# Building the state-space tables of a hybrid encoder block on one engine: two tables in one set of operations, half of a third one mirrored

## The chip, the cores and the metric

The kernel runs on one core of a Trainium2 chip. The metric is the device time of one execution in microseconds (us); the kernel before takes 1011.92 us, the median of three runs (1011.55 to 1013.5). The engines are named as in the profile: PE (TensorE matmuls; PEld its weight loads), DVE (VectorE), ACT (ScalarE), POOL (GpSimd) and SP (the queue that issues most transfers).

## The reference

One layer, one sequence of 1024 tokens, model width 1024. Two branches share one input projection: differential attention with 4 heads, and a bidirectional S5 state-space branch. Only the second is touched here:

```python
# 2 directions, 32 groups of 16 channels, 64 complex states each
mag = exp(lr * dt); ab = mag * (cos(li*dt) + i sin(li*dt))      # the state matrix's diagonal a
bb  = coef[..., None] * b                                        # input matrix
bu  = einsum('bsgh,gph->sbgp', u, bb)
x   = associative_scan(x[s] = a * x[s-1] + bu[s])                # per direction, one reversed
y   = einsum('sbgp,ghp->bsgh', x_re, c_re) - einsum('sbgp,ghp->bsgh', x_im, c_im)
```

The sum over both directions goes through D*u, GELU, a gate and an up-projection, is merged with the attention branch, and a last projection, residual and RMSNorm give the output.

## The kernel before

The program is written as generators that are stepped in an order fixed by hand: every engine runs its own instructions in program order. `drive(main, fill)` steps a main generator; each number that it yields is a budget of PE time, and that much of a second generator, `fill`, is put into the program at that place. The fill of the state-space stage are projection units: 48 matmuls each (16 steps of three, 0.66 of budget a step) that have nothing to do with the state-space work. Each unit's weights are split into a high part (ACT, tile `wh`) and a low part (in this stage DVE, tile `wl`) when the unit before it starts. So PE has work wherever the main line waits for another engine, as far as the budgets reach, and waits where they end.

The state-space work has two parts.

`startup` prepares parameters (`params_a` to `params_d`, `put_tabs`). `params_b` makes small tables of powers of a on DVE: `wn` (8 powers), `rbn` (16) and `ran` (8) unit rotations, the last from nine squarings (`e_pow`). `params_d` multiplies b by the coefficients (`bb`, six complex-product steps on POOL) and by a rotation (`bq`, six on DVE); `put_tabs` copies the tables with ACT to `wt`, `rb`, `ra`, with the second 64 partitions (the reversed direction) in reversed order; four ACT copies fill `bz` from `bb`.

`ssm_main` then handles eight blocks of four groups. A token index is split in 8 by 128 (T=8, NJ=128): within the 8 a small table does the work, over the 128 a scan. For block i:

- `stage_a`: three outer products of 128x512 elements, as six element-wise operations each (real and imaginary part: two products and a sum). `ba` (the B table, bq times wt) is made on DVE, `ca` (the C table, ct times wt) and `rr` (the rotation table, ra times rb) on POOL. ACT fills `rt`, POOL sets two of its columns.
- `stage_b`: PE transposes `ba` (tile `tp`), ACT copies the result to `gt`.
- `stage_k`: PE multiplies `bz` by `ca` (tile `kp`), ACT copies `kp` to `kt`, DVE and ACT form `kf` from it; by way of DRAM it comes back as the Toeplitz tile `m`.
- `stage_c`: PE multiplies `gt` by the input `ut` (PSUM tile `w`), DVE turns it by `rr` (six operations), runs four scans (`sb`) and two small memsets.
- `stage_d`: DVE turns the scans back by `rr` (six operations on `z` and `t`).
- `stage_e`: PE sums `m` times `ut` and `ca` times `z` (tile `yp`), ACT writes `ys`, and it goes to DRAM.

The order of the main line in iteration i is: stage_a(i+1), input load of i+1, stage_c(i), fill YA (4.4), stage_b(i+1), stage_e(i-1), fill YB (4.6), stage_d(i), stage_k(i+1), fill YC (4.6). So DVE's order in one iteration is ba(i+1), turning and scans of i, z of i, kf(i+1), with `wl` wherever a new unit starts; PE's order is w(i), YA, tp(i+1), yp(i-1), YB, kp(i+1), YC. Ahead of the loop stand stage_a(0), a fill of 7.0, stage_b(0), a fill of 5.0 and stage_k(0). The helper `tt` (L60) issues nearly all element-wise operations, and `act` (L81) all of ACT's, so the tiles' names tell them apart.

## Time and profile before

| | before |
|---|---|
| median of three runs | 1011.92 us |
| the profiled execution's own time | 1012.06 us |
| its span, first to last instruction | 1010.2 us |
| PE busy | 901.7 us (89%) |
| DVE busy | 710.0 us (70%) |
| POOL busy | 393.2 us (39%) |
| ACT busy | 375.9 us (37%) |
| granted PE clock, mean | 0.944 |
| chain that ended last | PE 52%, DVE 27%, ACT 6%, DMA 5% |

The shares are means over stages that differ. The startup lasts to about 120 us, the state-space stage with its fill from there to about 395 us; attention and the output projection follow. A row of the trace gives the start of an instruction, its duration, engine, line, operation and tiles; in brackets stands the idle time of the engine before it and what ended it. Where two operations of an engine follow each other closely, their durations overlap a little, and the distance of their starts is what the second costs.

### The profile page before, as it was taken

Reading aid. Unit: us, or ns where it says so; the run is one execution under the profiler, and the core shown is the slowest. Engines: PE = TensorE matmul, PEld = TensorE weight load, DVE = VectorE, ACT = ScalarE, POOL = GpSimd, SP = SyncE. Lnnn points to the kernel's source line nnn. Section 1 sums busy time; section 2 is a strip of 40 time slices with the busy share of each in tenths; the row PEclk is TensorE's granted clock in tenths of the full one; section 3 lists DMA queues with packets and bytes.
Section 4 is the critical chain, followed back from the end, with each engine's and each line's share of the span. In section 5 each row is a group of like instructions: output and inputs, shape, how many; then the busy total and the mean of one; then the engine's idle time right before and its main releaser. Section 6 shows DMA issues by size and latency. Waiting matters only on the chain.

```text
span 1010.2 us, 12306 instructions
## 1 busy us (share of the span) xinstructions
PE 901.7 (89%) x4532; PEld 751.3 (74%) x4532; DVE 710.0 (70%) x1179; ACT 375.9 (37%) x647; POOL 393.2 (39%) x250
## 2 busy tenths in 40 slices
PE   4699968588677799999989999899989999999997
PEld 3577856477566588787868888788878888788886
DVE  4984968999999987765646655856766563565455
ACT  5434351112111115511245545545545644332222
POOL 3433279876766801422226334515601110331000
PEclk9789988798777889999999999999999999999999
DMA  9744213022421425686343312131240231675212
GB/s 303 190 124 124 85 55 102 21 71 71 130 58 47 138 81 167 209 285 235 84 115 74 94 42 74 43 102 34 63 115 21 72 97 63 241 259 207 105 63 104
DMA packets 105326, 115.38 MB, mean 114 GB/s; under 512 B 7459, under 2 KB 87568, under 8 KB 105266
## 3 DMA queue, kind: packets, MB, share of 16 engines
q1 hardware_dynamic: 103476, 109.88, 35.6%
q10 hardware_dynamic: 1614, 4.51, 1.1%
q8 instruction: 36, 0.59, 0.2%
q0 software_dynamic: 176, 0.20, 0.1%
q14 instruction: 24, 0.20, 0.1%
HBM read 76.36 MB, written 25.63 MB: 101 GB/s over the span
## 4 chain that ended last, share of the span: by engine, by line
PE 52%; DVE 27%; ACT 6%; DMA 5%; issue 4%; POOL 3%; SPq 2%; DVEq 0%; ACTq 0%; POOLq 0%
PE mm L202 27%; PE op L1843 8%; PE pv L1614 4%; DVE ba L60 4%; DVE z L60 2%; PE sc L1573 2%; DVE tv L60 2%; PE sc L1572 2%; DVE acc L78 2%; PE tp L1603 2%; DVE t L60 2%; PE u L785 1%; DVE sb L1174 1%; DVE sb L1172 1%; DVE wl L60 1%
## 5 line engine op out<-in xcount | busy, mean ns | idle before, releaser
L202 PE MATMUL mm<-hh,wh 128*128 128x512 f32 x592 | 240.5, 406 | 0.6 <-ACT o L81 0.6
L202 PE MATMUL mm<-hl,wh 128*128 128x512 f32 x592 | 233.8, 395 | 0.0
L202 PE MATMUL mm<-hh,wl 128*128 128x512 f32 x592 | 233.3, 394 | 0.0
L60 POOL TENSOR_TENSOR wl<-wr,wh 128x1024 fp32r<-128x1024 f32 x28 | 74.7, 2667 | 289.7 <-ACT wh L81 287.9
L202 PEld LDWEIGHTS mm<-hh,wh 128*128 128x128 f32 x592 | 113.5, 192 | 24.0 <-issue 1.4
L202 PEld LDWEIGHTS mm<-hh,wl 128*128 128x128 f32 x592 | 112.8, 191 | 24.6
L202 PEld LDWEIGHTS mm<-hl,wh 128*128 128x128 f32 x592 | 113.2, 191 | 21.4
L60 DVE TENSOR_TENSOR wtl<-tp,wth 128x512 fp32r<-128x512 f32 x64 | 41.2, 686 | 101.1 <-ACT wth L81 101.1
L81 ACT ACTIVATE e<-sc,nm 128x1024 f32<-128x1024 f32 x64 | 71.4, 1116 | 98.3 <-DVE nm L1574 98.3
L1574 DVE TENSOR_REDUCE nm<-sc 128x1 f32<-128x1024 f32 x64 | 75.3, 1217 | 10.5 <-PE sc L1573 10.3
L1116 PE MATMUL tp<-cst,ba 128*128 128x128 f32 x64 | 16.9, 418 | 61.3 <-DVE ba L60 61.3
L81 ACT ACTIVATE wh<-wr 128x1024 fp32r<-128x1024 f32 x48 | 50.7, 1056 | 40.2 <-DMA pad<-pt 21.2
L1116 PEld LDWEIGHTS tp<-cst,ba 128*128 128x128 f32 x64 | 11.1, 212 | 67.3 <-issue 58.1
L1573 PE MATMUL sc<-kk,qb 128*128 128x512 f32 x128 | 50.3, 393 | 2.8 <-DMA qb<-qq 2.8
L1843 PE MATMUL op<-woh,ml 128*128 128x512 f32 (+1 forms) x136 | 51.7, 380 | 0.1
L1843 PE MATMUL op<-wol,mh 128*128 128x512 f32 (+1 forms) x136 | 51.6, 379 | 0.0
L1843 PE MATMUL op<-woh,mh 128*128 128x512 f32 (+1 forms) x136 | 51.6, 379 | 0.0
L1572 PE MATMUL sc<-kk,qq 128*128 128x512 f32 x128 | 50.2, 392 | 0.5 <-issue 0.5
L81 ACT ACTIVATE side<-mm 128x512 f32<-128x512 f32 x40 | 23.8, 595 | 68.0 <-PE mm L202 65.6
L78 DVE SCALAR_TENSOR_TENSOR e<-e,wm 128x1024 f32<-128x1024 f32 x32 | 47.1, 1472 | 1.1
L60 DVE TENSOR_TENSOR wl<-wr,wh 128x1024 fp32r<-128x1024 f32 x21 | 33.7, 1605 | 18.6 <-ACT wh L81 18.4
L60 POOL TENSOR_TENSOR ca<-ct,wt 128x512 f32<-128x512 f32 x16 | 28.0, 1750 | 39.2 <-PE yp L1200 34.3
(372 smaller groups left out, 2050.0 us busy)
## 6 DMA issues: line engine op xcount, KB each, us to landing
wr<-in_w_in_dram SPq DMA_DIRECT2D x40, 512.0 KB
wa<-in_w_ada_dram SPq DMA_DIRECT2D x16, 512.0 KB
x<-in_x_dram SPq DMA_DIRECT2D x8, 512.0 KB
gsd<-side SPq DMA_DIRECT2D x8, 512.0 KB
gad<-side SPq DMA_DIRECT2D x8, 512.0 KB
gt<-gsd SPq DMA_DIRECT2D x8, 512.0 KB
wg<-in_w_ada_dram SPq DMA_DIRECT2D x8, 512.0 KB
pad<-pt ACTq DMA_DIRECT2D x8, 512.0 KB
```

The source lines that it names most:

```text
L60: (e or V).tensor_tensor(out=o, in0=a, in1=b, op=op)
L78: V.scalar_tensor_tensor(out=o, in0=a, scalar=s, in1=b, op0=op0, op1=op1)
L81: A.activation(out=o, in_=i, func=f, **kw)
L202: PE.matmul(out=ps, lhsT=a[:, k, off:off + P], rhs=r[:, k, sl], start=(n == 0), stop=(n == 3 * K - 1))
L785: PE.matmul(out=upd[2 * b + hf], lhsT=w[:, k, :], rhs=r[:, k, hf * 512:hf * 512 + 512], start=(k == 0 and p == 0), stop=(k == KD - 1 and p ...
L1116: PE.transpose(ps[:, c4 * P:c4 * P + P], ba[:, q, c4].rearrange("p t h -> p (t h)"), ident)
L1572: PE.matmul(out=sc[:, sl], lhsT=H["qq"][:, cc, tok], rhs=H["kk"][:, cc, sl], start=True, stop=False)
L1573: PE.matmul(out=sc[:, sl], lhsT=qb_t[g // 2][:, cc, tb], rhs=H["kk"][:, cc, sl], start=False, stop=True)
L1574: V.tensor_reduce(out=nm[:, cc:cc + 1], in_=sc, axis=AX.X, op=ALU.max, negate=True)
L1603: PE.transpose(ps[:, k, :], e[:, kt * P:kt * P + P], ident)
L1614: PE.matmul(out=ps[:, 0:256], lhsT=a[:, kt, :], rhs=r[:, kt, :], start=(n == 0), stop=(n == 23))
L1843: PE.matmul(out=ps[:, 0:n], lhsT=a[:, k, tok], rhs=r[:, k, lo:lo + n], start=(i == 0), stop=(i == 23))
```

## The change

- In `stage_a` all three tables are made on DVE. B and C go through one set of six operations of 128x1024 elements: their sources lie interleaved in one tile `bc` (tile `bct`, last index 0 for B, 1 for C), and the result is one tile `cb`, interleaved too. PE reads `cb[..., 0]` and `cb[..., 1]`, each second element. Of `rr` DVE makes half (128x256 elements, six operations), and two ACT operations write the other half in reversed order, the imaginary part with its sign changed. POOL keeps the two small memsets.
- `ran` and `ra` shrink from 8 to 4 entries, with one squaring less; `put_tabs` changes signs instead of order for `rb` and `ra` (eight ACT operations for six).
- `bb` in `params_d` moves from POOL to DVE. Signs that were in `ct` move into `bz` and into stages c and d (an add for a sub and the reverse).
- `stage_k` loses the copy `kt`: DVE and ACT read `kp` in PSUM.
- `gt` has one buffer for two, `cb` three as `ca` had; `tv` shares a buffer with `t1`.

```diff
+            es, half = [], []
 
             def e_pow():
                 cur = (co, sn)
                 t0 = sb("et0")
-                for q in range(9):
+                for q in range(8):
                     nxt = (sb(f"er{q}"), sb(f"ei{q}"))
                     yield from csq(nxt[0], nxt[1], cur[0], cur[1], t0)
                     cur = nxt
                     if q >= 2:
                         es.append(nxt)
+                    if q == 1:
+                        half.append(nxt)
...
-            def r_tab(tab, q, tmp):
-                seed(tab, es[q])
-                yield from grow(tab, 2, es[q + 1], tmp)
-                yield from grow(tab, 4, es[q + 2], tmp)
-                if tab is rbn:
-                    yield from grow(tab, 8, es[3], tmp)
+            def r_tab(tmp):
+                seed(rbn, es[0])
+                for q in range(3):
+                    yield from grow(rbn, 2 << q, es[q + 1], tmp)
+
+            def h_tab(tmp):
+                for q in range(2):
+                    V.tensor_copy(out=ran[:, q, 0], in_=half[0][q])
+                yield from grow(ran, 1, es[4], tmp)
+                yield from grow(ran, 2, es[5], tmp)
...
-            ra = sp.tile([P, 2, 8, 32], F32, name="ra")
-            for dst, nm in ((wt, "wn"), (rb, "rbn"), (ra, "ran")):
+            ra = sp.tile([P, 2, 4, 32], F32, name="ra")
+            act(wt[0:64], small["wn"][0:64], AF.Copy)
+            act(wt[64:P], small["wn"][64:P, :, ::-1, :], AF.Copy)
+            yield 4.0
+            for dst, nm in ((rb, "rbn"), (ra, "ran")):
                 src = small[nm]
-                act(dst[0:64], src[0:64], AF.Copy)
-                act(dst[64:P], src[64:P, :, ::-1, :], AF.Copy)
-                yield 4.0 if dst is wt else 0.1
+                act(dst[:, 0], src[:, 0], AF.Copy)
+                act(dst[0:64, 1], src[0:64, 1], AF.Copy)
+                act(dst[64:P, 1], src[64:P, 1], AF.Copy, scale=-1.0)
...
-                act(ct[:, i], ps[:].rearrange("p (g h) -> p g h", h=16), AF.Copy, scale=(1.0 if i == 0 else -1.0))
+                act(bc_[:, i, :, :, 1], ps[:].rearrange("p (g h) -> p g h", h=16), AF.Copy)
...
-            bq = sp2[0].tile([P, 2, 32, 16], F32, name="bq")
-            cmul(bb[:, 0], bb[:, 1], bs[:, 0], bs[:, 1], bc(small["cr"][:], 1, shp), bc(small["ci"][:], 1, shp), tbig, G)
-            cmul(bq[:, 0].rearrange("p g h -> p h g"), bq[:, 1].rearrange("p g h -> p h g"), bb[:, 0], bb[:, 1],
+            cmul(bb[:, 0], bb[:, 1], bs[:, 0], bs[:, 1], bc(small["cr"][:], 1, shp), bc(small["ci"][:], 1, shp), tbig, V)
+            cmul(bc_[:, 0, :, :, 0].rearrange("p g h -> p h g"), bc_[:, 1, :, :, 0].rearrange("p g h -> p h g"), bb[:, 0], bb[:, 1],
...
-                    act(bz[64 * d:64 * d + 64, i, :, d, :], bb[64 * d:64 * d + 64, i].rearrange("p h g -> p g h"), AF.Copy)
-            tabs.update(bq=bq)
+                    act(bz[64 * d:64 * d + 64, i, :, d, :], bb[64 * d:64 * d + 64, i].rearrange("p h g -> p g h"), AF.Copy,
+                        scale=1.0 - 2.0 * i)
...
-        def outer(o, br, bi, wr, wi, im_sign, tmp, e):
-            mul(o[:, 0], br, wr, e)
-            mul(tmp, bi, wi, e)
-            tt(o[:, 0], o[:, 0], tmp, ALU.subtract if im_sign > 0 else ALU.add, e)
-            mul(o[:, 1], bi, wr, e)
-            mul(tmp, br, wi, e)
-            tt(o[:, 1], o[:, 1], tmp, ALU.add if im_sign > 0 else ALU.subtract, e)
+        def outer(o_r, o_i, br, bi, wr, wi, tmp):
+            mul(o_r, br, wr)
+            mul(tmp, bi, wi)
+            sub(o_r, o_r, tmp)
+            mul(o_i, bi, wr)
+            mul(tmp, br, wi)
+            add(o_i, o_i, tmp)
 
         def stage_a(i):
             g = slice(4 * i, 4 * i + 4)
-            ca = hb.tile([P, 2, 4, 8, 16], F32, tag="ca", bufs=3, name="ca")
+            cb = hb.tile([P, 2, 4, 8, 16, 2], F32, tag="cb", bufs=3, name="cb")
             rr = hb.tile([P, 2, 4, 8, 16], F32, tag="rr", bufs=2, name="rr")
-            ba = hb.tile([P, 2, 4, 8, 16], F32, tag="ba", bufs=1, name="ba")
-            tg = hb.tile(s4, F32, tag="tg", bufs=1, name="tg")
-            tv = hb.tile(s4, F32, tag="tv", bufs=1, name="tv")
+            tv = hb.tile([P, 4, 8, 32], F32, tag="t1", bufs=1, name="tv")
             rt = hb.tile([P, 4, P], F32, tag="rt", bufs=2, name="rt")
-
-            def wv(q):
-                return bc(wt[:, q, :, g].rearrange("p k g -> p g k"), 3, s4)
-
-            outer(ba, bc(bq[:, 0, g], 2, s4), bc(bq[:, 1, g], 2, s4), wv(0), wv(1), 1, tv, V)
-            outer(ca, bc(ct[:, 0, g], 2, s4), bc(ct[:, 1, g], 2, s4), wv(0), wv(1), -1, tg, G)
-            rv = [bc(ra[:, q, :, g].rearrange("p k g -> p g k"), 3, s4) for q in range(2)]
-            rw = [bc(rb[:, q, :, g].rearrange("p k g -> p g k"), 2, s4) for q in range(2)]
-            outer(rr, rv[0], rv[1], rw[0], rw[1], 1, tg, G)
+            sc, sr = [P, 4, 8, 32], [P, 4, 4, 16]
+            bv = [bc(bct[:, q, g].rearrange("p g h x -> p g (h x)"), 2, sc) for q in range(2)]
+            wv = [bc(wt[:, q, :, g].rearrange("p k g -> p g k"), 3, sc) for q in range(2)]
+            cf = cb[:].rearrange("p q g t h x -> p q g t (h x)")
+            outer(cf[:, 0], cf[:, 1], bv[0], bv[1], wv[0], wv[1], tv)
+            rv = [bc(ra[:, q, :, g].rearrange("p k g -> p g k"), 3, sr) for q in range(2)]
+            rw = [bc(rb[:, q, :, g].rearrange("p k g -> p g k"), 2, sr) for q in range(2)]
+            outer(rr[:, 0, :, 4:8], rr[:, 1, :, 4:8], rv[0], rv[1], rw[0], rw[1], tv[:, :, 0:4, 0:16])
+            for q in range(2):
+                f = rr[:, q].rearrange("p g a b -> p g (a b)")
+                act(f[:, :, 0:64][:, :, ::-1], f[:, :, 64:P], AF.Copy, scale=1.0 - 2.0 * q)
             act(rt, bc(r8[:, g], 2, [P, 4, P]), AF.Copy)
             G.memset(rt[0:64, :, 0:1], 0.0)
             G.memset(rt[64:P, :, P - 1:P], 0.0)
-            st_[i] = dict(ca=ca, rr=rr, ba=ba, rt=rt)
+            st_[i] = dict(cb=cb, rr=rr, rt=rt)
...
-            gt = hb.tile([P, 2, 4, P], F32, tag="gt", bufs=2, name="gt")
+            cb = d["cb"]
+            gt = hb.tile([P, 2, 4, P], F32, tag="gt", bufs=1, name="gt")
             for q in range(2):
                 ps = psw.tile([P, 512], F32, tag="tp", bufs=2, name="tp")
                 for c4 in range(4):
-                    PE.transpose(ps[:, c4 * P:c4 * P + P], ba[:, q, c4].rearrange("p t h -> p (t h)"), ident)
+                    PE.transpose(ps[:, c4 * P:c4 * P + P], cb[:, q, c4, :, :, 0].rearrange("p t h -> p (t h)"), ident)
...
-                              rhs=ca[:, q, c4].rearrange("p t h -> p (t h)"), start=(q == 0), stop=(q == 1),
+                              rhs=cb[:, q, c4, :, :, 1].rearrange("p t h -> p (t h)"), start=(q == 0), stop=(q == 1),
                               tile_position=(0, 32 * c4))
-            kt = hb.tile([P, P], F32, tag="kt", bufs=1, name="kt")
             kf = hb.tile([P, 240], F32, tag="kf", bufs=1, name="kf")
-            act(kt, kp, AF.Copy)
-            V.stream_shuffle(out=kf[:, 0:P], in_=kt, mask=SWAP16)
-            act(kf[:, P:240], kt[:, 16:P], AF.Copy)
-            add(kf[:, 112:P], kf[:, 112:P], kt[:, 0:16])
+            V.stream_shuffle(out=kf[:, 0:P], in_=kp, mask=SWAP16)
+            act(kf[:, P:240], kp[:, 16:P], AF.Copy)
+            add(kf[:, 112:P], kf[:, 112:P], kp[:, 0:16])
...
-            mul(wv[:, 1], wp[1], rre)
-            mul(t1, wp[0], rim)
+            mul(wv[:, 1], wp[0], rim)
+            mul(t1, wp[1], rre)
...
-            sub(z[:, 0], z[:, 0], t1)
+            add(z[:, 0], z[:, 0], t1)
             mul(z[:, 1], sv[:, 1], rre)
             mul(t1, sv[:, 0], rim)
-            add(z[:, 1], z[:, 1], t1)
+            sub(z[:, 1], z[:, 1], t1)
...
-                    PE.matmul(out=yp[:, c4, :], lhsT=ca[:, q, c4].rearrange("p t h -> p (t h)"),
+                    PE.matmul(out=yp[:, c4, :], lhsT=cb[:, q, c4, :, :, 1].rearrange("p t h -> p (t h)"),
```

## Rows read from the trace of the kernel before

**Rows 1.** Windows (busy us by engine, granted clock, DMA): an iteration, a later stretch.

```profile
303.01:333.12 30.11, 23.07 (x124) 19.55 (x123) 29.58 (x30) 5.52 (x10) 20.64 (x15) 0.83 0.23 66
...
400.00:450.00 50.00, 48.98 (x219) 39.09 (x218) 33.43 (x42) 18.06 (x25) 20.25 (x10) 1.00 0.70 235
```

**Rows 2.** Timelines of DVE and POOL (start, us, engine, line, operation).

```profile
316.53 1.73 DVE L60 TENSOR_TENSOR ba<-ba,tv 128x512 f32<-128x512 f32 x1
...
321.76 0.69 DVE L60 TENSOR_TENSOR ba<-ba,tv 128x512 f32<-128x512 f32 x1
...
319.58 1.59 POOL L60 TENSOR_TENSOR rr<-rr,tg 128x512 f32<-128x512 f32 x1
...
328.64 1.11 POOL L60 TENSOR_TENSOR ca<-ct,wt 128x512 f32<-128x512 f32 x1 [7.28 <-PE yp L1200]
```

**Rows 3.** Tile wv: least, median and greatest ns, all eight blocks.

```profile
L60 DVE TENSOR_TENSOR wv<-w,rr x16: 678/683/692, 168.5 to 373.1; 128x512 f32<-128x512 f32 x16
L60 DVE TENSOR_TENSOR wv<-wv,t x16: 691/692/1836, 169.8 to 374.5; 128x512 f32<-128x512 f32 x16
```

**Rows 4.** DVE timeline: first operations of stage_a(1) and stage_a(7).

```profile
159.71 0.68 DVE L60 TENSOR_TENSOR ba<-bq,wt 128x512 f32<-128x512 f32 x1
...
345.38 1.75 DVE L60 TENSOR_TENSOR ba<-bq,wt 128x512 f32<-128x512 f32 x1
```

**Rows 5.** DVE timeline: iteration 6, turning to turning.

```profile
353.58 0.68 DVE L60 TENSOR_TENSOR wv<-w,rr 128x512 f32<-128x512 f32 x1
...
357.43 1.21 DVE L1172 TENSOR_TENSOR_SCAN sb<-rt,wv 64x512 f32<-64x512 f32 x1
...
365.22 1.23 DVE L60 TENSOR_TENSOR wl<-wr,wh 128x1024 fp32r<-128x1024 f32 x1 [2.57 <-ACT wh L81]
366.36 0.69 DVE L60 TENSOR_TENSOR z<-sb,rr 128x512 f32<-128x512 f32 x1
...
370.23 0.30 DVE L1133 STREAM_SHUFFLE kf<-kt 128x128 f32<-128x128 f32 x1
...
370.91 0.69 DVE L60 TENSOR_TENSOR wv<-w,rr 128x512 f32<-128x512 f32 x1
```

**Rows 6.** DVE timeline, startup: an operation of 128x256.

```profile
124.02 0.41 DVE L60 TENSOR_TENSOR rbn<-rbn,er 128x256 f32<-128x256 f32 x1
```

**Rows 7.** Timelines of POOL, DVE and PE, from the parameters to stage_b(0).

```profile
121.78 5.49 POOL L60 TENSOR_TENSOR tbig<-bs,ci 128x512 f32<-128x512 f32 x1 [2.62 <-ACT bs L81]
...
125.36 0.75 DVE L60 TENSOR_TENSOR rbn<-rbn,tb 128x256 f32<-128x256 f32 x2
129.80 1.08 DVE L60 TENSOR_TENSOR bq<-bb,fr 128x512 f32<-128x512 f32 x1 [3.69 <-POOL bb L60]
133.31 0.69 DVE L60 TENSOR_TENSOR tbig<-bb,fi 128x512 f32<-128x512 f32 x1 [2.43 <-POOL bb L60]
...
137.66 1.22 DVE L60 TENSOR_TENSOR wl<-wr,wh 128x1024 fp32r<-128x1024 f32 x1
...
143.71 1.09 PE L1116 MATMUL tp<-cst,ba 128*128 128x128 f32 x4 [4.94 <-DVE ba L60]
148.31 1.12 PE L1116 MATMUL tp<-cst,ba 128*128 128x128 f32 x4 [3.51 <-DVE ba L60]
```

**Rows 8.** PE timeline without the fill, last two iterations.

```profile
353.81 1.09 PE L1116 MATMUL tp<-cst,ba 128*128 128x128 f32 x4 [1.91 <-DVE ba L60]
...
364.21 0.67 PE L1126 MATMUL kp<-ca,bz 128*32 128x128 f32 x16
369.75 1.95 PE L1157 MATMUL w<-ut,gt 128*128 128x128 f32 x16
376.32 0.38 PE L1198 MATMUL yp<-ut,m 128*128 128x128 f32 x2
```

**Rows 9.** Tile bn: weight loads from each sixteenth element, duration in ns.

```profile
L614 PEld LDWEIGHTS tp<-cst,bn x32: 182/200/206, 115.2 to 120.8; 32*128 32x128 f32 x32
```

**Rows 10.** ACT timeline: a copy of 128x512.

```profile
304.77 0.62 ACT L81 ACTIVATE rt<-r 128x512 f32<-128x512 f32 x1
```

More of the change, by code (lines that the diff above doesn't have):

```diff
@@ L513, in w_tab @@
                 yield from grow(wn, 4, a4, tb)
-            es = []
+            es, half = [], []
             def e_pow():
@@ L537, in params_b @@
             rbn = s2p[0].tile([P, 2, 16, 32], F32, name="rbn")
-            ran = s2p[0].tile([P, 2, 8, 32], F32, name="ran")
+            ran = s2p[0].tile([P, 2, 4, 32], F32, name="ran")
             tc_ = [s2p[0].tile([P, 4, 32], F32, name=f"tc{i}") for i in range(2)]
-            def r_tab(tab, q, tmp):
-                seed(tab, es[q])
-                yield from grow(tab, 2, es[q + 1], tmp)
-                yield from grow(tab, 4, es[q + 2], tmp)
-                if tab is rbn:
-                    yield from grow(tab, 8, es[3], tmp)
+            def r_tab(tmp):
[7 more added lines that the diff above has]
+                yield from grow(ran, 2, es[5], tmp)
             fr, fi = sb("fr"), sb("fi")
@@ L559, in f_gen @@
                 yield
-            for _ in rr_merge(r_tab(rbn, 0, tb), r_tab(ran, 4, tc_), f_gen()):
+            for _ in rr_merge(r_tab(tb), h_tab(tc_), f_gen()):
                 yield 0.4
@@ L570, in put_tabs @@
             rb = sp.tile([P, 2, 16, 32], F32, name="rb")
[L571 to L572 removed]
+            ra = sp.tile([P, 2, 4, 32], F32, name="ra")
[3 more added lines that the diff above has]
+            for dst, nm in ((rb, "rbn"), (ra, "ran")):
                 src = small[nm]
[L574 to L576 removed]
+                act(dst[:, 0], src[:, 0], AF.Copy)
+                act(dst[0:64, 1], src[0:64, 1], AF.Copy)
+                act(dst[64:P, 1], src[64:P, 1], AF.Copy, scale=-1.0)
+                yield 0.1
             tabs.update(wt=wt, rb=rb, ra=ra)
@@ L605, in params_c @@
             bs = s2.tile([P, 2, 16, 32], F32, name="bs")
-            ct = sp2[0].tile([P, 2, 32, 16], F32, name="ct")
+            bc_ = sp2[0].tile([P, 2, 32, 16, 2], F32, name="bc")
             bz = sp2[0].tile([P, 2, 32, 2, 16], F32, name="bz")
@@ L619, in params_c @@
                     PE.transpose(ps[:, P * q:P * q + P], cn[i][:, q].rearrange("r d p -> r (d p)"), ident)
-                act(ct[:, i], ps[:].rearrange("p (g h) -> p g h", h=16), AF.Copy, scale=(1.0 if i == 0 else -1.0))
+                act(bc_[:, i, :, :, 1], ps[:].rearrange("p (g h) -> p g h", h=16), AF.Copy)
                 yield 0.5
             small["bs"] = bs
-            tabs.update(ct=ct, bz=bz)
+            tabs.update(bc=bc_, bz=bz)
         def params_d():
             s2 = s2p[0]
-            bs, bz = small["bs"], tabs["bz"]
+            bs, bz, bc_ = small["bs"], tabs["bz"], tabs["bc"]
             bb = s2.tile([P, 2, 16, 32], F32, name="bb")
@@ L1067, in ssm_main @@
         psw = tc.alloc_tile_pool(name="ps_ssm", bufs=1, space=PSUM, side="right")
-        wt, rb, ra, ct, bq, bz, dd, r8 = (t[k] for k in ("wt", "rb", "ra", "ct", "bq", "bz", "dd", "r8"))
-        s4 = [P, 4, 8, 16]
+        wt, rb, ra, bct, bz, dd, r8 = (t[k] for k in ("wt", "rb", "ra", "bc", "bz", "dd", "r8"))
         st_ = {}
-        def outer(o, br, bi, wr, wi, im_sign, tmp, e):
-            mul(o[:, 0], br, wr, e)
-            mul(tmp, bi, wi, e)
-            tt(o[:, 0], o[:, 0], tmp, ALU.subtract if im_sign > 0 else ALU.add, e)
-            mul(o[:, 1], bi, wr, e)
-            mul(tmp, br, wi, e)
-            tt(o[:, 1], o[:, 1], tmp, ALU.add if im_sign > 0 else ALU.subtract, e)
+        def outer(o_r, o_i, br, bi, wr, wi, tmp):
[5 more added lines that the diff above has]
+            add(o_i, o_i, tmp)
@@ L1121, in stage_k @@
             d = st_[i]
-            ca = d["ca"]
+            cb = d["cb"]
             kp = psw.tile([P, P], F32, tag="k", bufs=1, name="kp")
@@ L1182, in stage_d @@
             d = st_.pop(i)
-            sv, rre, rim, ut, ca, m = (d[k] for k in ("sv", "rre", "rim", "ut", "ca", "m"))
+            sv, rre, rim = (d[k] for k in ("sv", "rre", "rim"))
             z = hb.tile([P, 2, 4, P], F32, tag="z", bufs=1, name="z")
@@ L1187, in stage_d @@
             mul(t1, sv[:, 1], rim)
-            sub(z[:, 0], z[:, 0], t1)
+            add(z[:, 0], z[:, 0], t1)
             mul(z[:, 1], sv[:, 1], rre)
             mul(t1, sv[:, 0], rim)
-            add(z[:, 1], z[:, 1], t1)
+            sub(z[:, 1], z[:, 1], t1)
             return d, z
         def stage_e(i, d, z):
-            ut, ca, m = d["ut"], d["ca"], d["m"]
+            ut, cb, m = d["ut"], d["cb"], d["m"]
             yp = psw.tile([P, 4, P], F32, tag="y", bufs=1, name="yp")
```

1 line of the change is left out of this document (removed).

## The prediction

> **What bounds the kernel now.** I read the page's slices first: PE is dense nearly everywhere except between 150 and 360 us, where DVE stands at nine or ten tenths. The windows say the same in numbers: in one iteration of 30.1 us DVE is busy 29.58, PE 23.07 at a mean granted clock of 0.83, so part of it at the lower of its two levels (1.2 of 2.4 GHz); after the stage PE is busy 48.98 of 50 us at 1.00 [rows 1]. So DVE sets the period of the eight blocks, PE the rest, and time taken out of DVE's chain here reaches the end: what follows is PE's own queue, which starts earlier as a whole. PE's waits name the place: its transposes wait for `ba`, still 1.91 us in iteration 6 [rows 8].
>
> Why DVE is so busy is in the timelines. The same operation on 512 elements takes 1.73 us while POOL works and 0.69 us in a gap of POOL's, which begins when POOL's tables of a block end [rows 2]. The tile's summary gives the condition: `wv` from PSUM and `rr` takes 678 to 692 ns in all sixteen cases, while `wv` from two SBUF tiles takes 691 to 1836 [rows 3]. So it is not the shape; two SBUF inputs beside a busy POOL cost about 1 us more.
>
> **The period after, worked out.** Six periods lie between the first operations of stage_a(1) and stage_a(7): 345.38 - 159.71 = 185.67 us, 30.9 each [rows 4]. After the change POOL has only two tiny memsets a block. What DVE then pays is seen in iteration 6, behind whose `ba` POOL has run dry [rows 5]:
> - turning by `rr`, six operations: 357.43 - 353.58 = 3.85; the six of `z`: 370.23 - 366.36 = 3.87.
> - four scans and memsets: 365.22 - 2.57 (idle) - 357.43 = 5.22.
> - `kf`: 370.91 - 370.23 = 0.68 (now from PSUM; the turning, from PSUM too, pays no more, so nothing is added).
> - one `wl`, 1024 elements: 366.36 - 365.22 = 1.14. A fill is seven steps, three fills are 21, a unit 16: 1.3 `wl` a period, 1.48.
> - B and C together, six operations of 1024: from 512 to 1024 an operation grows by 1.23 - 0.69 = 0.54, so 3.85 + 6 x 0.54 = 7.09. This replaces the six of `ba`.
> - half of `rr`, six of 256: 3.85 - 6 x 0.27 = 2.25; a 128x256 operation takes 0.41, which is 0.27 under the 0.68 of 512 [rows 6, 5].
>
> Sum 3.85 + 3.87 + 5.22 + 0.68 + 1.48 + 7.09 + 2.25 = 24.4 us. DVE does more work than before and still takes 6 us less a period.
>
> **Who is late next.** PE. Its way in the last iterations, from the second half of the transposes: 353.81 to 364.21 for tp, yp and YB, 0.67 for kp, to 369.75 for YC, 1.95 for w, to 376.32 for YA [rows 8]: 22.5 us, with tp and yp at the lower clock level (yp shorter behind YA). Another 0.6 us for the first half of the next transposes make 23.1, under 24.4, so DVE still leads by about 1.3 us. The reverse waits have room: kf needs kp 11.1 us after `cb` ends, and DVE comes there after rr, turning, scans and z, 15.2 us; the turning needs w after 17.9, DVE comes after 24.4 + 2.25. Only `wl` may wait when a unit starts late in YB: it waited 2.57 us in iteration 6, and the 2.25 of rr now lie ahead of it. I allow 0.3 us a period: 24.7, six are 148.2, **gain 37.5**.
>
> **The smaller terms.**
> - Startup. `bb` on POOL begins its last five operations at 121.78, the first of them 5.49 us, and DVE waits 3.69 and 2.43 us for it. DVE's own tables end at 126.1 [rows 7]; a squaring, shorter `ran` and no stretched operation beside POOL take off between 0.5 and 2.1, I say 1.5: 124.6. Then bb 3.85, bq 1.08 + (137.66 - 133.31) = 5.4, wl 1.14, cb(0) 7.09: 142.1. Before, the second transposes began at 148.31. **Gain 6.2.** Writing `bq` in steps of two elements is unknown; it already writes in long steps at 1.08, and I take that; the ends are 0.69 and twice that. PE had its fill done at 143.71 - 4.94 = 138.8, so it is no earlier bound.
> - From there to stage_a(1) the fill of 5.0 runs partly at the lower clock after two waits of 4.94 and 3.51; they shrink to about 3 together. No kt copy, no stretched kf: **gain 2.2** of 0 to 3.5.
> - Stage_a(7): 353.58 - 345.38 = 8.2 against 7.09 [rows 4, 5]: **1.1**. The yp behind it at the lower clock: **1** of 0 to 2.
> - At nothing: PE reads `cb` in steps of two elements. The nearest rows are weight loads in steps of 16 elements, 182 to 206 ns [rows 9], and I take nothing. If a tenth of a us were added to each of the 32 a period, that would be 3 us, of which DVE's lead of 1.3 covers a part; 10 us over the stage are the upper end. The mirrors, two on ACT of 256 elements, under 0.62 each [rows 10]: they wait for DVE's rr(i+1), and behind them in ACT's queue stand `rt`, evacuations, `wh` and `gt`; ACT is busy 5.5 of 30 us, rr(i+1) is used a period later, and PE has two PSUM banks for the fill. If a bank ran dry, PE would lose up to 2.25 us a period. No DMA moves and SP's and POOL's queues lose nothing they need: POOL's memsets of `rt` now wait for the mirrors alone. `gt` with one buffer is written after w has read it, by PE's order.
>
> **Sum:** 37.5 + 6.2 + 2.2 + 1.1 + 1 = 48.0. The profiled execution took 1012.06 (span 1010.2), 0.14 above the median 1011.92; 1012.1 - 48.0 = 964.1, so **964 us**.
>
> **Rivals.**
> - PE becomes the bound: if one fill block a period runs at the lower level, it costs 4.8 us more, the period is about 28, the gain 185.7 - 168 + 8 = 26, **986 us**. For it: 0.83 [rows 1]. Against: YB ran at the full level behind 1.91 us of waiting [rows 8], and waits get shorter. 0.06.
> - POOL was not the reason, and the wide operations keep the stretched price per element. `ba` took 8.2 us; cb would take 16.4 and half of rr 4.1, on top of 30.1 - 8.2: 42.4, six periods 74 us more, **1086 us**, slower. It decides from the point where over half of the 11 us of stretch in a period (30.1 less the unstretched 18.7) stays. Against: [rows 2, 3]. 0.03.
>
> The Trainium skill (Perfetto Trace Analysis, section on optimizing Scalar/DVE operations) speaks for this rival: a saturated DVE may be relieved by ScalarE or GPSIMD, and this change loads the saturated engine. It adds itself that shifting between these two might not help because of the shared port; by the first half 1086 is the time, by the second 964, and the rows are with the second.
>
> - The change doesn't do what it says: the stage gets shorter but the tail waits for something that did not move (weights, the outputs' way through DRAM), the time stays within 0.2%, about what a measurement of this kernel can tell from no change. PE's 48.98 of 50 [rows 1] speaks against it. 0.02.
>
> **How the numbers follow.** Forecast 0.89, the rest as above. Low end: no wait for wl, 39.3 + 7.4 + 3.5 + 1.1 + 2 = 53.3 and some tenths a period of unknown prices: 957. High end: the 10 us of PE's reads, or a period of 26.5 through waits (26.7 + 8 + 1.1 = 36): 977. The cases outside hold under 2 in 10. Faster 0.95, same 0.02, slower 0.03.
>
> **What would show it.** Right: iterations of 24 to 25 us with DVE over 95% busy, cb at 1.22 us, every `z` and scan at 0.69 and 1.22, PE still waiting 1 to 3 us at tp for cb, first transposes some 6 us earlier. Wrong: cb well above 1.3 us, DVE idle for kp or w (then PE or ACT bounds), PE idle for a bank behind the mirrors, or a clock in the iterations still at 0.83.

## The result and the profile after

The changed kernel takes **984.38 us** (median of four runs, 982.57 to 985.13) against 1011.79 for the kernel before in the same series: ratio 0.9717, 95% interval 0.970 to 0.9734. The direction was right; the gain is 27.4 us where 48.0 were forecast, and 984 lies above the range of 957 to 977.

| | before | after |
|---|---|---|
| span of the profiled execution | 1010.2 us | 980.8 us |
| PE busy | 901.7 us (89%) | 896.3 us (91%) |
| DVE busy | 710.0 us (70%) | 672.4 us (69%) |
| POOL busy | 393.2 us (39%) | 214.7 us (22%) |
| granted PE clock, mean | 0.944 | 0.964 |

The windows of the kernel after, in the form of [rows 1], are two periods, ten microseconds behind the state-space stage, and the later stretch:

```profile
256.14:281.30 25.16, 22.61 (x136) 18.84 (x135) 24.22 (x36) 5.00 (x11) 0.20 (x2) 1.00 0.28 79
281.30:308.71 27.41, 23.89 (x133) 20.13 (x134) 25.41 (x38) 6.70 (x13) 0.20 (x2) 0.94 0.31 96
370.00:380.00 10.00, 6.58 (x21) 5.25 (x22) 2.10 (x3) 3.66 (x4) 3.37 (x2) 0.66 0.62 233
400.00:450.00 50.00, 49.99 (x219) 38.41 (x218) 28.45 (x38) 6.75 (x8) 12.50 (x7) 1.00 0.74 263
```

The period is shorter and DVE still leads it, busy for 24.22 of 25.16 us; one period in three, the one with a second `wl`, takes 27.4 us. New is the third row: PE idles a third of ten microseconds and its granted clock falls to 0.66. One period of after in DVE's timeline, as in [rows 2, 5]:

```profile
256.14 1.22 DVE L60 TENSOR_TENSOR cb<-bc,wt 128x1024 f32<-128x1024 f32 x1
...
263.20 0.60 DVE L60 TENSOR_TENSOR rr<-ra,rb 128x256 f32<-128x256 f32 x1
...
264.36 0.43 DVE L60 TENSOR_TENSOR rr<-rr,tv 128x256 f32<-128x256 f32 x1
...
266.21 0.69 DVE L60 TENSOR_TENSOR wv<-w,rr 128x512 f32<-128x512 f32 x1
...
270.06 1.21 DVE L1178 TENSOR_TENSOR_SCAN sb<-rt,wv 64x512 f32<-64x512 f32 x1
...
276.45 0.69 DVE L60 TENSOR_TENSOR z<-sb,rr 128x512 f32<-128x512 f32 x1
...
280.33 0.30 DVE L1139 STREAM_SHUFFLE kf<-kp 128x128 f32<-128x128 f32 x1
281.00 0.17 DVE L60 TENSOR_TENSOR kf<-kf,kp 128x16 f32<-128x16 f32 x1 [0.38 <-ACT kf L81]
...
281.30 1.22 DVE L60 TENSOR_TENSOR cb<-bc,wt 128x1024 f32<-128x1024 f32 x1
```

The six of `cb` take 263.20 - 256.14 = 7.06 (forecast 7.09), and `z` and the scans are at 0.69 and 1.21. But half of `rr` takes 266.21 - 263.20 = 3.01 instead of 2.25, its products 0.60 against 0.43 for the sums, and `kf` now waits for ACT. In the six periods, from 153.25 to 308.71 us, DVE's waits come to 4.4 us (a row of waits gives the total in us, how often, and the longest):

```profile
DVE kf L60 <- ACT kf L81: 2.3, 6, 0.4
DVE wl L60 <- ACT wh L81: 2.1, 2, 1.1
```

ACT's waits, from 150 to 320 us:

```profile
ACT rr L81 <- DVE rr L60: 70.9, 14, 9.9
ACT kf L81 <- issue: 37.4, 4, 10.6
ACT kf L81 <- DVE kf L1139: 21.7, 3, 9.0
```

ACT stands some 10 us a block at the mirrors, and again at its own part of `kf`, behind DVE's shuffle: both read `kp` now, and the shuffle stands first in the program. (In the rows "issue" means that the profile names nothing that ACT waited for; e3_kf_first will show what these waits hang on.) In the kernel before, ACT had only PE to wait for at this place, from 150 to 395 us:

```profile
ACT kt L81 <- PE kp L1126: 15.5, 4, 6.3
```

Behind ACT's part of `kf` in its queue stand evacuations (its copies that empty PE's PSUM banks) and `wh`. The mirrors show their price at the startup, in the timelines of ACT, PE and DVE:

```profile
140.51 0.74 PE L1124 MATMUL tp<-cst,cb 128*128 128x128 f32 x4 [2.72 <-DVE cb L60]
...
142.07 0.42 ACT L81 ACTIVATE rr<-rr 128x256 f32<-128x256 f32 x1 [8.80 <-issue]
...
144.98 0.80 PE L202 MATMUL mm<-hh,wh 128*128 128x512 f32 x1 [2.66 <-ACT side L81]
...
147.37 1.23 DVE L60 TENSOR_TENSOR wl<-wr,wh 128x1024 fp32r<-128x1024 f32 x1 [3.89 <-ACT wh L81]
```

The stretch of the third window row is this, in the timelines of PE, POOL and SP:

```profile
373.43 0.80 PE L202 MATMUL mm<-yh,wl 128*128 128x512 f32 x1 [6.46 <-POOL wl L60]
...
365.50 5.57 POOL L60 TENSOR_TENSOR zt<-zt,ye 128x1024 f32<-128x1024 f32 x2 [2.30 <-DMA zt<-zsd]
371.04 2.34 POOL L60 TENSOR_TENSOR wl<-wr,wh 128x1024 fp32r<-128x1024 f32 x1
...
364.26 0.43 SPq L159 DMA_DIRECT2D wr<-in_w_glu_dram  x1
```

PE waits 6.46 us for `wl`, which POOL makes behind the products `zt`. In the kernel before, POOL did them the other way round:

```profile
392.45 2.42 POOL L60 TENSOR_TENSOR wl<-wr,wh 128x1024 fp32r<-128x1024 f32 x1 [40.48 <-ACT wh L81]
...
405.23 6.66 POOL L60 TENSOR_TENSOR zt<-zt,ye 128x1024 f32<-128x1024 f32 x2 [3.24 <-DMA zt<-zsd]
```

The diff touches neither. But every yield of the parameters' generators is a piece of the fill's budget, and a squaring less is two yields of 0.25 less. So the fill lags one step of three matmuls from there on. The start of its last unit, which asks for the first weights of the gate (the GLU weights), then falls out of the state-space stage, and in the queues it comes behind the next stage's first instructions.

The theory is this: the stretch of DVE's operations beside POOL is what the change removes, and the missing 20 us are four things beside it, namely the lag of the fill, the order at `kf`, the step in `rb` and the mirrors' place. The rival for each is that TensorE or the next wait takes over when it is mended.

The table gives the runs in stages, each from one profiled execution's timelines: a(i) is DVE's first operation of stage_a(i), "six periods" a(1) to a(7), "rest" a(7) to the span's end. The columns differ in how far they can be read. The six periods repeat within 0.2 us (155.46 to 155.61 in after, e2, e6 and e14). But a(0) lies anywhere between 132.0 and 136.2 in the kernels with the changed parameters, and no edit explains that; and the rest lies between 662.1 and 669.0 in the nine kernels without the lag.

| kernel | median us | ratio, interval | a(0) | a(0) to a(1) | six periods | rest |
|---|---|---|---|---|---|---|
| before | 1011.79 | | 138.79 | 20.92 | 185.67 | 664.8 |
| after | 984.38 | 0.9717 (0.9700-0.9734) | 133.31 | 19.94 | 155.46 | 672.1 |
| e1_align | 973.99 | 0.9636 (0.9605-0.9668) | 131.98 | 20.43 | 156.66 | 662.5 |
| e2_glu_dve | 983.9 | 0.9725 (0.9701-0.9750) | 134.50 | 20.69 | 155.57 | 671.9 |
| e3_kf_first | 981.66 | 0.9706 (0.9677-0.9736) | 136.20 | 19.88 | 151.21 | 672.4 |
| e4_before_shift | 1019.32 | 1.0073 (1.0047-1.0098) | 136.90 | 20.93 | 185.64 | 674.0 |
| e5_rb_layout | 980.38 | 0.9689 (0.9666-0.9713) | 133.87 | 20.13 | 151.05 | 673.8 |
| e6_glu_queues | 979.24 | 0.9676 (0.9654-0.9698) | 134.98 | 20.64 | 155.61 | 665.3 |
| e7_rr_pool | 980.74 | 0.9691 (0.9664-0.9719) | 135.52 | 20.61 | 156.36 | 669.0 |
| e8_three | 968.64 | 0.9566 (0.9538-0.9595) | 134.37 | 20.18 | 146.81 | 666.9 |
| e9_mirror_late | 962.32 | 0.9516 (0.9479-0.9553) | 133.04 | 16.75 | 146.82 | 662.8 |
| e10_pool_reads | 1011.73 | 1.0003 (0.9987-1.0018) | 133.10 | 19.97 | 188.65 | 669.0 |
| e11_pool_memset | 962.11 | 0.9514 (0.9489-0.9539) | 133.26 | 16.77 | 146.95 | 662.1 |
| e12_before_vec | 987.68 | 0.9763 (0.9746-0.9780) | 137.09 | 15.05 | 170.24 | 663.7 |
| e13_pool_narrow | 996.96 | 0.9859 (0.9841-0.9877) | 134.19 | 17.90 | 174.96 | 667.2 |
| e14_mirror_alone | 982.17 | 0.9709 (0.9688-0.9730) | 135.33 | 16.75 | 155.54 | 675.2 |

### The profile page after: what moved, and what is told of

Same layout as the page of the kernel before. It is cut to its first block, busy times and chain, and to the rows that moved or that the text cites. A ratio compares the mean times of both kernels' runs of the same rounds, so it can differ in the third digit from the quotient of the medians.

```text
span 980.8 us, 12246 instructions
## 1 busy us (share of the span) xinstructions
PE 896.3 (91%) x4532; PEld 746.0 (76%) x4532; DVE 672.4 (69%) x1229; ACT 376.1 (38%) x657; POOL 214.7 (22%) x146
## 4 chain that ended last, share of the span: by engine, by line
PE 53%; DVE 16%; ACT 7%; issue 6%; DMA 2%; POOL 2%; SPq 1%; ACTq 0%; DVEq 0%
PE mm L202 30%; PE op L1849 9%; DVE cb L60 4%; PE pv L1620 4%; DVE tv L60 3%; PE sc L1579 2%; PE sc L1578 2%; PE tp L1609 2%; ACT jk L81 2%; DVE rr L60 1%; PE yp L1206 1%; DVE rq L60 1%; POOL wl L60 1%; ACT wh L81 1%; ACT e L81 1%
## 5 line engine op out<-in xcount | busy, mean ns | idle before, releaser
L202 PEld LDWEIGHTS mm<-hh,wh 128*128 128x128 f32 x592 | 112.9, 191 | 30.9 <-ACT side L81 7.1
L60 DVE TENSOR_TENSOR wtl<-tp,wth 128x512 fp32r<-128x512 f32 x64 | 41.2, 686 | 101.4 <-ACT wth L81 101.4
L81 ACT ACTIVATE wh<-wr 128x1024 fp32r<-128x1024 f32 x48 | 50.8, 1059 | 47.2 <-DVE pt L78 16.4
L60 DVE TENSOR_TENSOR wl<-wr,wh 128x1024 fp32r<-128x1024 f32 x21 | 28.0, 1331 | 26.7 <-ACT wh L81 26.5
L81 ACT ACTIVATE rr<-rr 128x256 f32<-128x256 f32 x16 | 6.7, 417 | 80.7 <-DVE rr L60 71.9
L81 ACT ACTIVATE wth<-tp 128x512 fp32r<-128x512 f32 x64 | 34.7, 596 | 7.2 <-PE tp L1609 5.8
L1124 PE MATMUL tp<-cst,cb 128*128 128x128 f32 x64 | 13.1, 337 | 26.0 <-DVE cb L60 26.0
```

The lines of the kernel that those rows point to most:

```text
L60: (e or V).tensor_tensor(out=o, in0=a, in1=b, op=op)
L81: A.activation(out=o, in_=i, func=f, **kw)
L202: PE.matmul(out=ps, lhsT=a[:, k, off:off + P], rhs=r[:, k, sl], start=(n == 0), stop=(n == 3 * K - 1))
L1124: PE.transpose(ps[:, c4 * P:c4 * P + P], cb[:, q, c4, :, :, 0].rearrange("p t h -> p (t h)"), ident)
```

## The experiments

**The lag of the fill.** Put back, in the changed kernel:

```diff
             for _ in rr_merge(coef(), w_tab(), e_pow(), r8_gen()):
                 yield 0.25
+            yield 0.25
+            yield 0.25
```

> The changed kernel with two more yields of 0.25 at the end of the tables of powers, so that the fill again stands one step further ahead, as in the kernel before (its ninth squaring paid these two yields). Theory A: the fill's lag of one step moves the split of the first GLU weights on POOL behind the products zt, which wait for a transfer; PE then waited 6.46 us and came back at the lower clock. Expected 984.4 - 7.5 = 977 us (974 to 979), PE's wait for POOL wl gone. Rival: the way of the last block through DRAM (yd, yt, zt) sets the start of the GLU whatever POOL's order is; then the wait only changes its name and the time stays at 983 to 986.

Measured 973.99: the rest goes from 672.1 to 662.5 us and nothing else moves by more than 1.4. PE's wait for POOL's `wl` is gone; from 330 to 440 us this alone is left:

```profile
PE mm L202 <- ACT sg L81: 2.0, 2, 1.3
```

The same from the other side, in the kernel before (the ninth squaring stays, its yields go):

```diff
-                    yield from csq(nxt[0], nxt[1], cur[0], cur[1], t0)
+                    if q == 8:
+                        run_all(csq(nxt[0], nxt[1], cur[0], cur[1], t0))
+                    else:
+                        yield from csq(nxt[0], nxt[1], cur[0], cur[1], t0)
```

> The kernel before with the yields of its ninth squaring taken out (the squaring itself stays), so that its fill lags by the same step as in the changed kernel and the GLU split falls behind zt on POOL; no other part of the change. Theory A: slower by what the tail of the changed kernel lost, 1011.8 + 7 = 1019 us (1016 to 1021). Rival (the loss comes from the new tables or from DRAM's way): 1011 to 1013.

Measured 1019.32, 7.1 us above the kernel before in the same series (1012.23), and the wait is there, among PE's waits:

```profile
PE mm L202 <- POOL wl L60: 6.2, 1, 6.2
```

Over all runs, the six that have the lag (after, e2 to e5 and e14; e6 below stands apart) show a rest of 671.9 to 675.2, the nine without it 662.1 to 669.0.

The next runs ask through which queue the lag costs, and keep it. First POOL's queue alone: `w_state["eng"] = V` at the start of the next stage lets DVE make the first GLU `wl`.

> The changed kernel, its fill as it is, but the split of the first GLU weights is made by DVE instead of POOL (the engine is switched at the start of the stage after the blocks). Theory A: POOL's queue order is the cause, so the 6.46 us wait goes with it: 977 us (974 to 980), though the fill still lags by a step. If it is the lag itself that costs and not the queue, 983 to 986.

Measured 983.9, not the 977 expected: POOL is out of it and nothing is won, for PE now waits as long for ACT. PE's and ACT's waits behind the stage:

```profile
PE mm L202 <- ACT sg L81: 6.0, 1, 6.0
...
ACT wh L81 <- DMA wr<-in_w_glu_dram: 7.8, 1, 7.8
```

ACT waits for the second GLU weights, whose load stands on SP behind those of `yt`, `zt` and `gt`. So POOL's order is not the whole cause. The next run frees both queues, with `w_load()` issued there too:

```diff
+        w_state["eng"] = V
+        w_load()
```

> The changed kernel with the lag of the fill (three matmuls of the last unit left over at the end of the state-space stage) kept, but with both queues behind it freed at the start of the next stage: the splits of the first GLU weights go to VectorE, and the second of their loads is issued on SyncE before the loads of yt, zt and gt. Theory: the lag costs through these two queues and no other way: the 6 us wait of TensorE goes and the time is near that of the kernel with the two yields put back, 976 us (973 to 979). Rival: the three matmuls themselves, or ScalarE's place in the order, are what costs: 982 to 986, with TensorE waiting 5 us or more for something else at 365 to 380 us.

Measured 979.24, a little above the range expected; its stage began 1.7 us later than after's. The rest is 665.3, so of the 9.6 us of lag the two queues hold 6.8. The other 2.8 are no more than the spread of the rest among the kernels without the lag, where 665.3 lies in the middle; whether anything else costs stays open.

**The order at kf.** In stage_k:

```diff
-            V.stream_shuffle(out=kf[:, 0:P], in_=kp, mask=SWAP16)
             act(kf[:, P:240], kp[:, 16:P], AF.Copy)
+            V.stream_shuffle(out=kf[:, 0:P], in_=kp, mask=SWAP16)
```

> The changed kernel with the two readers of kp in the other order: ACT's copy to kf ahead of DVE's shuffle. Theory B: ACT's copy waits for DVE's shuffle since the copy kt is gone, and ACT's queue (evacuations, wh) stands for up to 10 us a block behind it; DVE then waits 0.38 us a block for ACT, and twice 1.05 us for wh. Expected: these waits go, 6 x 0.38 + 2 x 1.1 and one to two us of PE waiting for evacuations, so 984.4 - 5 = 979 us (977 to 981), clean periods at 24.8 instead of 25.15. Rival: ACT has slack and DVE sets the period anyway; then only the 0.38 goes, 981 to 983.

Measured 981.66, which as a total lies in the rival's range, as a(0) came 2.9 us later here. The periods decide: the six lose 4.2 us where the rival gives 2.3, and the one in three goes from 27.4 to 26.0. That is DVE's 4.4 us of waits in the six periods, all of which are gone. ACT's waits at `kf`, 59.1 us in after, are 15.5.

**The step in rb.** `rb` as [2, 32, 16] instead of [2, 16, 32], written by the same ACT copies:

```diff
-            rb = sp.tile([P, 2, 16, 32], F32, name="rb")
+            rb = sp.tile([P, 2, 32, 16], F32, name="rb")
...
-            rw = [bc(rb[:, q, :, g].rearrange("p k g -> p g k"), 2, sr) for q in range(2)]
+            rw = [bc(rb[:, q, g], 2, sr) for q in range(2)]
```

> The changed kernel with one table laid out the other way: rb as [2, 32, 16] instead of [2, 16, 32], so that the operand of the four rotation products is read element by element instead of with a step of 32 elements. Theory: the step alone makes these products 0.60 us against 0.42 for the two sums beside them; here all six take 0.41 to 0.43, the half of rr takes 2.5 instead of 3.0 us, and since VectorE sets the period, six periods and stage_a(7) get about 0.6 to 0.75 shorter each: 979.5 us (978 to 982). Rival: the products are longer for another reason (the other operand is a broadcast too): still 0.60, 984. Second rival: the products get shorter but TensorE or ScalarE sets the period: 0.42 in the rows and 983 to 985.

Measured 980.38, with the six periods 4.4 us shorter. Grouped by line and shape (busy us, mean ns), from 180 to 330 us:

```profile
L60 DVE TENSOR_TENSOR rr<-rr,tv 128x256 f32<-128x256 f32 x12 | 5.1, 425 | 0.4
L60 DVE TENSOR_TENSOR rr<-ra,rb 128x256 f32<-128x256 f32 x12 | 5.0, 418 | 0.0
```

The products are now 418 ns, no longer than the sums: the step was the whole difference, and the other operand, a broadcast in both kernels, costs nothing.

**The three together.**

> The changed kernel with three things at once: the two yields that hold the fill in step, ScalarE's copy of kf ahead of VectorE's shuffle, and the rotation table without the step. If these three are the places where the forecast's 20 us went, and they add: 10.4 (alignment) + 2.7 (kf) + 4.5 (rotation products) below 984.4 = 967 us (964 to 970), near the forecast of 964. If TensorE's own queue takes over as the periods get shorter, the gains do not add: 970 to 974, with VectorE idle behind TensorE in the periods.

Measured 968.64. The gains nearly add, 15.7 of 17.1. The periods are 24.07 and 25.22 and their mean 24.47, beside 24.7 in the forecast. PE did not take over: in the six periods DVE waits for nothing.

**The mirrors' place.** Moved from behind DVE's products to behind the copies of `gt`, with the three:

```diff
-            for q in range(2):
-                f = rr[:, q].rearrange("p g a b -> p g (a b)")
-                act(f[:, :, 0:64][:, :, ::-1], f[:, :, 64:P], AF.Copy, scale=1.0 - 2.0 * q)
...
                 act(gt[:, q], ps[:].rearrange("p (c q) -> p c q", c=4), AF.Copy)
+            for q in range(2):
+                f = d["rr"][:, q].rearrange("p g a b -> p g (a b)")
+                act(f[:, :, 0:64][:, :, ::-1], f[:, :, 64:P], AF.Copy, scale=1.0 - 2.0 * q)
```

> The three changes of the run before, and ScalarE's two mirrors are issued after the copies of gt instead of ahead of rt, so that its queue does not stand behind VectorE's rotation products while TensorE's banks wait to be emptied. Theory: the waits of TensorE for ScalarE's evacuations (2.7 us at the startup, about 1 in two of the periods) go: 0 to 3 us below the run before, 965 us (962 to 968). Rival: the mirrors now come late for the products from PSUM, VectorE waits for them, and the periods are 0.5 us or more longer: 968 to 975.

Measured 962.32. ACT's wait at the mirrors, 70.9 us in after, is now this:

```profile
ACT rr L81 <- DVE rr L60: 2.0, 4, 0.5
```

The stretch from a(0) to a(1) falls from 20.18 to 16.75. The periods don't change, so in them the wait was hidden. The rest is 4.1 us shorter too, which is within its spread. The mirrors alone, moved in the changed kernel:

> The changed kernel with one thing moved: ScalarE's two mirrors are issued after the copies of gt instead of ahead of rt. Theory: in the changed kernel ScalarE stands at the first mirror while TensorE's banks fill; at the startup this costs the 3.2 us by which the kernel with the mirrors late and the three other repairs is shorter from cb(0) to cb(1) (16.75 against 19.94), and up to 1 us in two or three periods: 980 us (977.5 to 982). Rival: ScalarE stands in the same place anyway, at kf behind the shuffle, and nothing is won alone: 983 to 986.

Measured 982.17, just above the range expected, and too near to after's 984.38 for the total to say much. The stages say it: a(0) to a(1) is 16.75 instead of 19.94, again 3.2 us, and the six periods are the same (155.54 and 155.46). In the profiled execution an a(0) 2.0 later and a rest 3.1 longer hide the gain. So the mirrors cost by themselves, and at the startup only.

**Is it POOL?** The part of the change that only moves work, in the kernel before: `tg, G` becomes `tg, V` in the two outer products of `ca` and `rr`.

> The kernel before with one thing alone: the B and C tables and the whole rotation table, 18 operations of 128x512 in a block, all on VectorE, still in three sets and with nothing mirrored. VectorE gets 12 operations a period more. Theory (stretch): each of the 18 takes 0.69, 12.4 us a period, the other rows go back to their unstretched lengths, and the period is the 25.9 us of the changed kernel + 12.4 - 10.1 = 28.2 us against 30.9: 997 us (990 to 1002). Rival (VectorE sets the period and GpSimd's share was free): 12 x 0.69 = 8.3 us more a period, 1065 us or more.

Measured 987.68: there are 12 more operations on DVE in each period, and the period falls from 30.9 to 28.4 us. That is close to the 28.2 of the theory in part by luck. Four of the 18 have the step of `rb` and take 1.09 instead of 0.69, 1.6 us a period more; the 25.9 it started from held 0.7 us of waits that this kernel does not have, and six operations in a row take 3.85 and not 6 x 0.69. Most of the 9 us beyond the expectation are the startup, which it left out: a(0) comes 1.7 earlier, and a(0) to a(1) takes 15.05 instead of 20.92.

In the next two runs POOL gets work in the kernel with the mirrors late, with results that nobody uses. First products:

```diff
+            pd = hb.tile([P, 256], F32, tag="pd", bufs=1, name="pd")
+            wf_ = wt[:].rearrange("p q k g -> p (q k g)")
+            for _ in range(16):
+                mul(pd, wf_[:, 0:256], wf_[:, 256:512], G)
```

> The kernel of the mirrors issued late, with 16 products of 128x256 on GpSimd in each block, both operands from a table in SBUF, their result used by nobody (and one buffer instead of two for the output of a block, to make room). No instruction of another engine is added and none waits for these. Theory (two-operand work of GpSimd stretches that of VectorE): in the kernel before, some 21 us of such GpSimd work in a period went with about 15 us of stretch, 0.7 us per us; 16 products of about 0.8 us are 13 us, so the periods go from 24.4 to some 33 us, the products and scans from SBUF take 1.3 to 1.8 times as long in the rows, the products that read PSUM stay at 0.68, and the time is 1020 us (1005 to 1035). Rival (the gain came from fewer waits and operations, not from GpSimd's silence): 962 to 966, rows unstretched.

Measured 1011.73: all that the change and its repairs had gained is gone again. Grouped rows, 200 to 300 us:

```profile
L60 DVE TENSOR_TENSOR tv<-bc,wt 128x1024 f32<-128x1024 f32 x6 | 10.5, 1743 | 0.0
...
L60 DVE TENSOR_TENSOR rr<-ra,rb 128x256 f32<-128x256 f32 x6 | 5.7, 944 | 0.0
...
L60 DVE TENSOR_TENSOR wv<-w,rr 128x512 f32<-128x512 f32 x8 | 5.4, 681 | 0.0
...
L60 POOL TENSOR_TENSOR pd<-wt 128x256 f32<-128x256 f32 x48 | 56.8, 1183 | 3.8
```

Then 48 `G.memset(pd, 0.0)` in place of the products:

> As the run with the products, but GpSimd writes constants: 48 memsets of 128x256 in each block, which read nothing. Theory (it is two-operand reading from SBUF that stretches, not GpSimd being busy): VectorE's rows stay as they are without them (0.68 and 1.22) and the time is 962 to 966 us. Rival (any work on GpSimd, or its writes into SBUF, stretches VectorE): the same stretch per us of GpSimd work as in the run with the products, 1000 us or more.

Measured 962.11, with POOL busier than it was with the products:

```profile
L60 DVE TENSOR_TENSOR tv<-bc,wt 128x1024 f32<-128x1024 f32 x9 | 11.0, 1218 | 0.0
...
L60 DVE TENSOR_TENSOR rr<-ra,rb 128x256 f32<-128x256 f32 x8 | 3.3, 418 | 0.0
...
L1109 POOL MEMSET pd<- 128x256 f32 x201 | 62.7, 312 | 11.5
```

So it is neither POOL's being busy nor its writing. POOL's products, which read two inputs from SBUF, hold up DVE operations that have two inputs there, and leave `wv<-w,rr`, with one of its two in PSUM, at 681 ns. The tiles need not be shared: the products read `wt`, and `rr<-ra,rb` is held up too. A POOL instruction with a single input from SBUF was not run. The Trainium skill (SBUF — State Buffer, section Who interferes with whom) states the same condition, and that a GpSimd instruction which only writes is excepted; 418 ns beside the memsets and 944 beside the products agree.

**What work left on POOL costs.** Here the rotation table's part of the change is undone: all of `rr` on POOL, no mirrors, the tables and squarings of before, and at `kf` ScalarE first.

```diff
-            outer(rr[:, 0, :, 4:8], rr[:, 1, :, 4:8], rv[0], rv[1], rw[0], rw[1], tv[:, :, 0:4, 0:16])
...
+            for h in (slice(0, 4), slice(4, 8)):
+                outer(rr[:, 0, :, h], rr[:, 1, :, h], *[a[:, :, h] for a in rv + rw], tg, G)
```

> The changed kernel with the whole rotation table back on GpSimd as before (12 products and sums of 128x256 a block with the tables of before, nothing mirrored), ScalarE's copy of kf ahead of the shuffle, the ninth squaring and its yields kept, one buffer for the output of a block. VectorE loses 3.0 us of work a period. Theory (stretch): 12 operations of GpSimd, about 10 us a period at 0.7 us of stretch per us, give VectorE 7 us more: periods of 29 to 30 us, 998 us (990 to 1005). Rival (VectorE is the busiest engine of the stage, so what is taken off it comes out): periods of 22 to 23 us, 952 to 958.

Measured 980.74: theory and rival both missed. Three microseconds a period came off DVE, and the period did not fall to 22: it is 26.1 against 25.2 in e3_kf_first. But it did not reach 29 either. The stretch was 3.9 us a period, where a rate of 0.7 per us of POOL work asked for 7. The rows of e10_pool_reads suggest why: 0.42 became 0.94 and 1.22 became 1.74, both +0.52, and in before 0.69 became 1.73 [rows 2], +1.04, beside operations twice as wide. So the price may be one wait for each DVE operation. The test has 32 products of 128x128 in place of the 16 of 128x256:

> The run with unused products on GpSimd again, with 32 products of 128x128 in a block instead of 16 of 128x256: the same elements in twice as many instructions. In the rows so far a VectorE operation beside GpSimd is longer by the same amount whatever its own length: beside 128x256 products 0.42 becomes 0.94 and 1.22 becomes 1.74, both +0.52; beside 512-wide ones 0.69 becomes 1.73, +1.04. Theory (each VectorE operation with two SBUF inputs waits once, for one GpSimd instruction): beside 128x128 products it is +0.26: 0.68, 0.95 and 1.48 in the rows, about 25 such operations in a period, some 5 to 6.5 us, 1000 us (993 to 1008). Rival (the stretch goes with the time beside GpSimd, or with the elements that GpSimd reads): 1.22 becomes 1.74 again and 0.42 becomes about 0.6; the total stretch stays at 7 us a period or grows with the longer GpSimd work: 1010 to 1030.

Measured 996.96. Rows of its DVE timeline:

```profile
204.40 0.95 DVE L60 TENSOR_TENSOR t<-sb,rr 128x512 f32<-128x512 f32 x1
...
212.16 1.47 DVE L60 TENSOR_TENSOR tv<-bc,wt 128x1024 f32<-128x1024 f32 x1
...
213.66 1.36 DVE L60 TENSOR_TENSOR cb<-cb,tv 128x1024 f32<-128x1024 f32 x1
...
219.72 0.67 DVE L60 TENSOR_TENSOR tv<-ra,rb 128x256 f32<-128x256 f32 x1
```

The products go from 0.42 to 0.67, from 0.69 to 0.95 and from 1.22 to 1.47: +0.25 or +0.26 each, half of the +0.52 in e10_pool_reads, though POOL is busy for 91.8 of 100 us here and for 56.8 there. The rate is refuted, and one wait per operation stands for DVE's products. The sums, each behind the product that it reads, wait less: `cb<-cb,tv` goes from 1.22 to 1.36 here and to 1.63 in e10_pool_reads.

One operation does not fit. `wl` on DVE has two inputs in SBUF too and keeps its 1.23 us in both runs. The timelines of DVE and POOL in e13_pool_narrow show who waits:

```profile
202.38 1.23 DVE L60 TENSOR_TENSOR wl<-wr,wh 128x1024 fp32r<-128x1024 f32 x1
...
202.43 1.50 POOL L60 TENSOR_TENSOR pd<-wt 128x128 f32<-128x128 f32 x1
```

DVE began first, and POOL's product takes 1.50 us, where the shortest of its kind takes 0.454. So the wait goes both ways: the engine that begins first holds up the other.

## Why the prediction missed

| term | forecast | after | e9_mirror_late |
|---|---|---|---|
| six periods | 37.5 | 30.2 | 38.9 |
| startup and fill up to stage_a(1) | 8.4 | 6.5 | 9.9 |
| stage_a(7) | 1.1 | 1.1 | 1.1 |
| from there to the end | 1.0 | -8.4 | 0.9 |
| sum | 48.0 | 29.4 | 50.8 |

(Gains in span against before, from one execution each. The six of `cb` behind a(7) take 7.06 in both. The way from there to the end hangs on the rest, with its spread of 7 us, so that 0.9 beside 1.0 is luck.)

**Right.** The reading of [rows 2, 3], shown by e10 to e13; DVE's period as a sum of unstretched rows; `cb` at 7.06; PE under DVE, and its reads of `cb` in steps of two at nothing that reaches the period, which is 24.47 in e8: these held. Of the rivals, the first two did not come: the periods did not go to 28 and `cb` was not stretched. Of the third, a tail that waits for weights, the mechanism came, at 9.6 us instead of the whole gain. Relieving a saturated DVE by GPSIMD, the rule of the Trainium skill (Perfetto Trace Analysis, section on optimizing Scalar/DVE operations) behind the second rival, made the period 0.9 us longer in e7, as its caution on the shared port has it.

**Wrong, by weight.**
- "what follows is PE's own queue, which starts earlier as a whole", and "SP's and POOL's queues lose nothing they need": 9.4 us between the forecast gain of 1.0 and the loss of 8.4, shown by e1, e4 and e6. The step follows from the diff's instructions alone. But the yields of a removed step also pace the fill, and where its last unit starts decides what stands ahead of it in two queues.
- Half of `rr` at 2.25: it measured 3.01, 0.76 more a period. The row taken was a contiguous operation [rows 6], while the diff's operand has a step of 32 elements. e5 gave 4.4 us back.
- `kf`, "so nothing is added", and no `kt` copy as a pure gain: DVE's own time was right, but without `kt` ACT waits for DVE, and 4.2 us of the periods hang on that (e3). The forecast allowed 0.3 us a period for waits, 1.8 in all; they came to 4.4, those at `wl` among them.
- "From there to stage_a(1)" at a gain of 2.2: the mirrors were put at nothing, with up to 2.25 us a period if a bank ran dry. In the periods a price of nothing was right. At the startup a bank did run dry, PE's 2.66 us above, and it cost 3.2 us (e14). From the start of the second transposes (148.31 before, 140.51 in after, 140.24 in e9) to a(1) after loses 1.3 us, while e9 gains 1.9.
- Half of `rr` in stage_a(7) stands in no term. It filled time in which DVE idled 2.57 us before [rows 5], and no loss shows from it: from a(7) to the end of DVE's last `z` it is 41.2 us in before and 40.8 in after.

In the periods the account closes: after lies 7.3 us above the forecast 148.2, which is 4.6 for `rr` and 4.4 for the waits, less the 1.8 allowed. What the change itself holds was forecast well in the periods: with the four repaired the gain there is 38.9, beside 37.5. The whole gain of 50.8 (49.9 between the medians of that series) is as close to 48.0 in part by luck, as a(0) and the rest wander by several us; the startup's 6.2, which came as 7.8 in after, hangs on a(0) too. The range was too narrow for effects of order: beyond waits inside a period it held prices only.
